# A hybrid encoder block on one core: one chunk of the residual turned by DMA, and a rotation in two halves

## The chip, the core and the metric

The kernel runs on one core of a Trainium2 chip. Its engines work side by side, each through its own list of instructions: TensorE (PE: matmuls, and transposes as matmuls with an identity), VectorE (DVE), ScalarE (ACT), GpSimd (POOL) and SyncE (SP, which here only issues DMAs). ACT and POOL can issue DMAs too. The metric is the device time of one execution in microseconds (us); less is better. A time is the median of several runs, and one more execution is profiled.

## The reference

One encoder layer in float32 over 512 tokens of width 2048:

```
h = rmsnorm(x);  qA|kA|vA|qB|kB|vB = h @ W_in
A = grouped-query attention, 8 heads, q and k normed and axially rotated
B = dilated sliding-window attention, 8 heads, q and k partially rotated:
    only the first 32 of a head's 128 columns are turned by the angles
x1 = x + concat(rmsnorm(A), rmsnorm(B)) @ W_out
out = rmsnorm(x1 + SwiGLU(rmsnorm(x1)))
```

What matters here: x1 (512 x 2048) is needed transposed, features on the partitions, as the operand of the gate-up matmul; and q and k of B are needed transposed for the scores.

## The kernel before

Every float32 matmul is three matmuls (`mm3`, L227 to L231) of a high and a low part: `split` writes the high part on ACT (a rounding copy) and the low part on DVE (the difference). Weights are split the same way, unit by unit: `split_hi` (L302) on ACT and `split_lo` (L307) on DVE; in the gate-up stage two units at once (L904, L907), with a sum of two weight tiles before it (L1040) for most forms, since that stage multiplies by a seven-product scheme (m1 to m7).

The program is written out by hand. Its order comes from a list of **units**: one unit is one weight tile times all 512 rows, 12 matmuls for the projections (a chunk of 512 output columns has 16 units, in the output projection 8), 6 for a unit of the gate-up stage. `prepare(n)` issues ahead of unit n the weight splits of a unit that comes later (in the output projection: the high part of unit n + 3, then the low part of unit n + 2). Work that belongs to no unit stands in a queue named `side`: after each unit `give` takes tasks from its head, and outside the attention a unit has a credit of 1.0, a task costs 1.0 unless it says otherwise, and `wait(k)` puts in k empty tasks. Every engine runs its instructions in the order in which they are issued this way.

**Output projection of B.** Four chunks c = 0 to 3 of eight units. The document counts them U0 to U31, so chunk 0 ends in U7, chunk 1 in U15, chunk 2 in U23, chunk 3 in U31; the gate-up stage follows with G0, G1 and so on (G0 is what U32 would be). At the end of a chunk `post` (L1187) adds the four row tiles to x1 on DVE (L1192), squares them on ACT (L1144, not for chunk 3), and puts the chunk's tasks into `side`. For chunks 0 to 2 these are `h_side(i, part)` for two pairs of feature blocks, i = 2c and 2c + 1:

- part 0 and part 1: four transposes of 128 x 128 on PE (L1238) into a PSUM bank, then a copy with the gain on ACT into `hpart[0]` (L1241); part 1 also forms four sums on DVE (`pair_sums`, L380);
- part 2: the split of seven forms, two copies on ACT (L1249) and two differences on DVE (L1251), into the arena that the gate-up matmuls read.

`park_x1(c)` stores the chunk from SP. Chunk 3's tasks are finer: parts 2 and 3 are the copy and the difference. Before the change the tasks of chunk 0 fall to U9 to U14 after two empty ones, those of chunk 1 to U16 to U21, those of chunk 2 to U24 to U29, and those of chunk 3 start in G0. The gate-up stage reads pair q as m1, q = 0 to 5 in G0 to G5, as m2, q = 0 to 5 in G6 to G11, then m1, q = 6 and 7 in G12 and G13.

**Turning by DMA.** Some heads are turned by `class Turned` without PE: `part(t)` separates on ACT the 16-bit halves of a row tile (L551, into `plane`), `turn(t)` transposes them by a DMA on SP's queue (L556, into `words`), `merge(h)` puts the halves together again on ACT (L561). They are used for heads 2 to 7 of A and heads 4 to 7 of B; B's heads come in pairs j, so these are pair groups j = 2 and 3.

**Rotation.** `rope_partial` (L533) rotates a whole pair group with four DVE instructions (L538 twice, L541, L542). Heads are worked in slots; head h of B starts at slot s = 4(8 + h). For j = 2 and 3 the group is reloaded from DRAM at slot s - 15, rotated at s - 11, and its row tiles are turned from s - 10 on. During the attention a unit's credit is higher, and `prepare`, `head_slot` and these tasks share the engines with the output projection of A.

Of the kernel before, what the change touches and what calls it, by code (L numbers as in the profile page):

```python
# [11 lines left out]
F32 = mybir.dt.float32  # L12
# [8 lines left out]
P = 128  # L21
# [45 lines left out]
COLUMN_BLOCKS = 3  # L67
SUM_LEAD = 6
ATTEND_PAST = 4
TURNED_ON_PE = {"A": 2, "B": 4}  # L70


# [5 lines left out]
def encoder_block(ctx, tc, x, w_in, g_q_a, g_k_a, w_out, w_gate_up, w_down, g_final, x_t, gains, c_ident, c_mask,  # L78
# [11 lines left out]
    def nm(base):  # L90
        counter[0] += 1
        return f"{base}_{counter[0]}"

    def slot(base, dtype=F32, shape=(P, 512)):
        return sp.tile(list(shape), dtype, tag="s", name=nm(base))
# [224 lines left out]
    def wait(n):  # L320
        side.extend([lambda: None] * n)
# [56 lines left out]
    def form_sums(a_l, a_r, b_l, b_r, s1, s2, s3, s4):  # L378
        def tt(out, x, y, op=OP.subtract):
            nc.vector.tensor_tensor(out, x, y, op=op)  # L380
        tt(s1, a_r, b_r, OP.add)
        tt(s3, a_l, a_r)
        tt(s2, s1, a_l)
        tt(s4, b_l, s2)
# [112 lines left out]
    def reload(name, dst):  # L497
        assert stored[name] == NT, name
        whole = slot(name, F32, (P, NT, 512))
        nc.sync.dma_start(whole, spill[name].rearrange("t p c -> p t c"))  # L500
        dst.update((t, whole[:, t]) for t in range(NT))
        dst["whole"] = whole
# [27 lines left out]
    def split_vB(h):  # L530
        vB[h] = split(vB[h].rearrange("p t c -> p (t c)"), "v", at=heads[NHA + h].home("v"))

    def rope_partial(q):  # L533
        rot = q.rearrange("p t (h d) -> p t h d", h=4)[:, :, :, :PARTIAL]
        tmp = turning.rearrange("p (t h c) -> p t h c", t=NT, h=4)
        hp = PARTIAL // 2
        for s in range(2):
            nc.vector.tensor_tensor(  # L538
                tmp[:, :, :, s * hp:(s + 1) * hp], rot[:, :, :, (1 - s) * hp:(2 - s) * hp],
                ropeb[:, 1, :, s * hp:(s + 1) * hp][:, :, None, :].to_broadcast([P, NT, 4, hp]), op=OP.mult)  # L540
        nc.vector.tensor_tensor(rot, rot, ropeb[:, 0][:, :, None, :].to_broadcast([P, NT, 4, PARTIAL]), op=OP.mult)  # L541
        nc.vector.tensor_tensor(rot, rot, tmp, op=OP.add)  # L542

    class Turned:
# [5 lines left out]
            src = self.whole()[:, t].bitcast(U16).rearrange("p (h c s) -> p h s c", h=4, s=2)  # L550
            nc.scalar.activation(p.rearrange("p (h s c) -> p h s c", h=4, s=2), src, AF.Copy)  # L551

        def turn(self, t):
            if self.words is None:
                self.words = slot("words", U16, (P, NT, 8, P))
            nc.sync.dma_start_transpose(self.words[:, t], self.planes.pop(t))  # L556

        def merge(self, h):
            m = slot("merged")
            src = self.words[:, :, 2 * h:2 * h + 2].rearrange("p t s c -> p t c s")  # L560
            nc.scalar.activation(m.bitcast(U16).rearrange("p (t c s) -> p t c s", c=P, s=2), src, AF.Copy)  # L561
            return m

    turned_a = [Turned(lambda j=j: qA[j]["whole"]) for j in range(2)]
# [167 lines left out]
    def weighed(cost, f):  # L732
        f.cost = cost
        return f

    def light(cost, tasks):
        return [weighed(cost, f) for f in tasks]

    def attention_tasks():
        def q_tasks(j):  # L740
            return norm_rope(lambda t: (qA[j][t], qA[j][t]), 4, "q")

        def both(cost, *lists):
            return [weighed(cost, lambda fs=fs: [f() for f in fs]) for fs in zip(*lists)]

        qA.update({j: {} for j in range(2)})
        qkB.update({j: {} for j in range(4)})
        push_heads()
        k_squares, k_turned, k_scaled = norm_rope(lambda t: (kA[t][:, :256], kA[t][:, 256:]), NKV, "k")
        q_squares, q_turned, q_scaled = q_tasks(0)  # L750
        vs = [lambda t=t: split_vA(t) for t in range(NT)]
        tables = light(0.8, table_tasks())
        todo = tables[:3] + both(1.4, [lambda t=t: scale_k(t) for t in range(NT)], k_squares)
        todo += both(0.6, vs) + tables[3:]
        todo += both(2.0, q_squares, k_turned, k_scaled) + both(2.6, q_turned, q_scaled)
        todo += light(0.6, [lambda kv=kv: transpose_k_a(kv) for kv in range(NKV)]) + [heads[0].tq, heads[0].tk]
        todo += light(0.1, [lambda: reload("qA1", qA[1])])
        extra = {}

        def at(slot, tasks):  # L760
            extra.setdefault(slot, []).extend(tasks)
        at(20, light(0.1, [lambda: nc.sync.dma_start(mask, c_mask)]))
        q_squares, q_turned, q_scaled = q_tasks(1)
        for t in range(NT):
            at(t // 2, both(0.8, q_squares[t:t + 1]))
            at(2 + 2 * t, both(0.9, q_turned[t:t + 1]))
            at(3 + 2 * t, both(0.9, q_scaled[t:t + 1]))
        def turn_at(turned, slots):
            for t, s in enumerate(slots):
                at(s, light(0.05, [lambda t=t: turned.part(t)]))  # L770
                at(s + 1, light(0.05, [lambda t=t: turned.turn(t)]))
        turn_at(turned_a[0], (0, 1, 2, 2))
        turn_at(turned_a[1], range(4, 12, 2))
        for j in range(4):
            s = NT * (NHA + 2 * j)
            lead = 4 if 2 * j >= TURNED_ON_PE["B"] else 0
            at(s - 11 - lead, light(0.1, [lambda j=j: reload(f"qkB{j}", qkB[j])]))
            at(s - 7 - lead, light(0.9, [lambda j=j: rope_partial(qkB[j]["whole"])]))
            if lead:
                turn_at(turned_b[j], range(s - 10, s - 6))  # L780
        for h in range(NHB):
            s = NT * (NHA + h)
            at(s + 2, light(0.1, [lambda h=h: load_vB(h)]))
            at(s + 4, light(0.4, [lambda h=h: split_vB(h)]))
        for s in range(2 * NHA * NT + VALUE_LAG + 2):
            cost = 1.5 if s < NHA * NT else 1.2 if s < 2 * NHA * NT else 0.7
            todo += [weighed(cost, lambda s=s: head_slot(s))] + extra.get(s, [])
        return todo
# [357 lines left out]
    def out_chunk(kind, c):  # L1146
# [28 lines left out]
        def mm(u, n):  # L1175
            k = order[n]
            if n == 0:
                box["ps"] = [bank() for _ in range(NT)]
                if kind == "A":
                    whole = slot("x1", F32, (P, NT, 512))  # L1180
                    x1[c] = [whole[:, t] for t in range(NT)]
                    for t in range(NT):
                        nc.sync.dma_start(x1[c][t], x[0, t * P:(t + 1) * P, c * 512:(c + 1) * 512])
            by_rows(u, n, NHA, lambda i, w, t: mm3(box["ps"][t], cols(oS[kind, order[i]], t * P), w, i == 0,
                                                   i == NHA - 1), post, kind == "A")

        def post(rows):  # L1187
            drain_until(lambda: kind in ro)
            if (kind, c) == ("B", 0) and 0 in rows:
                nc.scalar.activation(slot("table")[:, :1], ones, AF.Silu)  # L1190
            for t in rows:
                nc.vector.scalar_tensor_tensor(x1[c][t], box["ps"][t], ro[kind][:, t:t + 1], x1[c][t],  # L1192
                                               op0=OP.mult, op1=OP.add)
                release(box["ps"][t])
                if kind == "B" and c < NC - 1:
                    square_x1(c, t)
            if kind == "B" and NT - 1 in rows:
                wait(2 if c == 0 else 1)
                if c == NC - 1:
                    side.extend(lambda p=p: h_side(2 * c, p, True) for p in range(4))  # L1200
                    side.append(lambda: [square_x1(c, t) for t in (0, 1)])
                    side.extend(lambda p=p: h_side(2 * c + 1, p, True) for p in range(2))
                    side.append(lambda: park_x1(c))
                    side.append(lambda: [square_x1(c, t) for t in (2, 3)])
                    side.extend(lambda p=p: h_side(2 * c + 1, p, True) for p in range(2, 4))
                    side.append(make_r2)
                    return
                for i in (2 * c, 2 * c + 1):
                    for part in range(3):
                        side.append(lambda i=i, part=part: h_side(i, part))  # L1210
                side.append(weighed(0.0, lambda: park_x1(c)))
# [7 lines left out]
    def park_x1(c):  # L1219
        for t in range(NT):  # L1220
            nc.sync.dma_start(x1_dram[c, t], x1[c][t])

    def pair_sums(w):
        def part(n):
            return w[:, n * 256:(n + 1) * 256]
        a_r, a_l, s3, s2, b_l, b_r, s1, s4 = (part(n) for n in range(8))
        form_sums(a_l, a_r, b_l, b_r, s1, s2, s3, s4)

    hf = [False] * (KD // 2)
    hpart = {}  # L1230
# [465 lines left out]
```

## Time and profile before

| | us |
|---|---|
| median of 3 runs | 1950.06 (1948.17 to 1950.37) |
| the profiled execution | 1950.34, its span 1948.5 |
| PE busy | 1933.7 |
| DVE busy | 1536.4 |
| ACT busy | 1153.9 |
| POOL busy | 140.8 |

The span is what lies between the first and the last profiled instruction; 1.8 us of the profiled time lie around it. PE's granted clock was 0.999 of full. A row of a timeline gives the start, the duration, the engine, the line, the tiles written and read and, in square brackets, the engine's idle time before it with what ended it. A row of a line's or a tile's view gives the count and the shortest, median and longest duration in ns. A row of the waits gives the total in us, how often, and the longest. "SPq" and "ACTq" are those engines' issuing of DMAs.

### The profile page before, as it was taken

The numbers are of one execution on the slowest core, as the hardware profiler recorded it, in microseconds if no ns is written. First come the engines' busy times: TensorE is split into PE (matmuls) and PEld (weight loads), VectorE is DVE, ScalarE is ACT, GpSimd is POOL, SyncE is SP. The second block draws the span as 40 slices with busy tenths as digits, with TensorE's granted clock in tenths as the row PEclk, the third lists the DMA queues.
The fourth block names the chain that finished last, engine by engine and source line by source line (L and its number), as shares of the span: only waits on it lengthen the run. The fifth ranks groups of instructions, "written<-read, shape, count | busy, mean of one in ns | idle before, by whom it ended". The sixth has DMA issues, their size and how long they took to land.

```text
span 1948.5 us, 24527 instructions
## 1 busy us (share of the span) xinstructions
PE 1933.7 (99%) x8687; PEld 1594.9 (82%) x8687; DVE 1536.4 (79%) x2012; ACT 1153.9 (59%) x1673; POOL 140.8 (7%) x184
## 2 busy tenths in 40 slices
PE   9999999999999999999999999999999999999998
PEld 7888887888788888888888888888888888888886
DVE  7887768887785697778778777787788978787886
ACT  7655556676665565555555555555565666565555
POOL 0000011000000000000000000000000121111121
PEclk9999999999999999999999999999999999999999
DMA  9676694345442556758757778678587799868865
GB/s 347 221 276 218 214 295 112 100 168 161 115 150 95 183 185 215 272 148 280 244 173 275 222 206 286 186 240 291 144 287 264 217 239 272 229 164 242 236 145 170
DMA packets 268924, 413.50 MB, mean 212 GB/s; under 512 B 75584, under 2 KB 102720, under 8 KB 268672
## 3 DMA queue, kind: packets, MB, share of 16 engines
q1 hardware_dynamic: 237968, 325.31, 51.9%
q0 software_dynamic: 22480, 60.57, 12.4%
q10 hardware_dynamic: 8352, 26.05, 4.0%
q8 instruction: 68, 1.11, 0.2%
q14 instruction: 56, 0.46, 0.1%
HBM read 334.52 MB, written 62.65 MB: 204 GB/s over the span
## 4 chain that ended last, share of the span: by engine, by line
PE 87%; issue 8%; DVE 2%; ACT 1%; POOL 1%; DMA 0%; ACTq 0%; DVEq 0%; POOLq 0%; SPq 0%
PE b L230 29%; PE b L231 29%; PE b L229 29%; PE b L659 1%; DVE x L1192 0%; PE b L1238 0%; POOL fixed L211 0%; PE b L857 0%; POOL qkB L482 0%; DVE tw L963 0%; DVE w L307 0%; DMA stage<-in_w_in_dram 0%; DVE pair L380 0%; ACT rj L448 0%; ACT arena L1249 0%
## 5 line engine op out<-in xcount | busy, mean ns | idle before, releaser
L904 ACT ACTIVATE wide<-raw 128x1024 fp32r<-128x1024 f32 x462 | 487.3, 1059 | 456.9 <-PE b L231 264.8
L907 DVE TENSOR_TENSOR wide<-raw,wide 128x1024 fp32r<-128x1024 f32 x462 | 562.4, 1222 | 200.0 <-ACT wide L904 191.8
L229 PE MATMUL b<-wide,arena 128*128 128x512 f32 x1848 | 719.6, 389 | 0.0
L231 PE MATMUL b<-wide,arena 128*128 128x512 f32 x1848 | 719.0, 389 | 0.0
L230 PE MATMUL b<-wide,arena 128*128 128x512 f32 x1848 | 718.9, 389 | 0.0
L231 PEld LDWEIGHTS b<-wide,arena 128*128 128x128 f32 x1848 | 346.8, 188 | 72.0
L229 PEld LDWEIGHTS b<-wide,arena 128*128 128x128 f32 x1848 | 346.9, 188 | 72.0
L230 PEld LDWEIGHTS b<-wide,arena 128*128 128x128 f32 x1848 | 346.9, 188 | 71.7
L1040 DVE TENSOR_TENSOR raw<-raw,raw 128x1024 f32<-128x1024 f32 x264 | 321.4, 1219 | 9.3 <-DMA raw<-in_w_gate_up_dram 9.3
L230 PE MATMUL b<-tw,arena 128*128 128x512 f32 x396 | 154.3, 390 | 0.6 <-DVE tw L963 0.6
L231 PE MATMUL b<-tw,arena 128*128 128x512 f32 x396 | 154.1, 389 | 0.0
L229 PE MATMUL b<-tw,arena 128*128 128x512 f32 x396 | 154.1, 389 | 0.0
L960 ACT ACTIVATE tw<-stage 128x512 fp32r<-128x512 f32 x140 | 85.5, 629 | 69.3 <-DVE stage L1040 44.4
L963 DVE TENSOR_TENSOR tw<-stage,tw 128x512 fp32r<-128x512 f32 x140 | 93.7, 687 | 23.6 <-ACT tw L960 22.8
L229 PE MATMUL b<-w,arena 128*128 128x512 f32 x240 | 95.3, 397 | 0.0
L231 PE MATMUL b<-w,arena 128*128 128x512 f32 x240 | 93.9, 391 | 0.0
L230 PE MATMUL b<-w,arena 128*128 128x512 f32 x240 | 93.5, 390 | 0.0
L230 PEld LDWEIGHTS b<-tw,arena 128*128 128x128 f32 x396 | 74.3, 188 | 16.8 <-DVE tw L963 1.4
L229 PEld LDWEIGHTS b<-tw,arena 128*128 128x128 f32 x396 | 74.3, 188 | 15.6
L231 PEld LDWEIGHTS b<-tw,arena 128*128 128x128 f32 x396 | 74.3, 188 | 15.3
L380 DVE TENSOR_TENSOR pair<-pair 128x256 f32<-128x256 f32 x120 | 46.4, 422 | 46.8 <-ACT pair L1241 23.2
L1342 POOL DMA_DIRECT2D forms<-pair x22 | 20.1, 915 | 776.8 <-DVE pair L380 751.1
(243 smaller groups left out, 2138.3 us busy)
## 6 DMA issues: line engine op xcount, KB each, us to landing
raw<-in_w_gate_up_dram SPq DMA_DIRECT2D x308, 512.0 KB, 6.2
raw<-in_w_down_dram SPq DMA_DIRECT2D x88, 512.0 KB, 7.5
stage<-in_w_in_dram SPq DMA_DIRECT2D x111, 256.0 KB, 5.4
forms<-pair POOLq DMA_DIRECT2D x22, 896.0 KB, 6.3
fr<-forms ACTq DMA_DIRECT2D x35, 512.0 KB, 5.9
raw<-in_w_out_dram SPq DMA_DIRECT2D x32, 512.0 KB, 4.2
x1d<-s POOLq DMA_DIRECT2D x54, 256.0 KB, 6.8
stage<-in_w_in_dram SPq DMA_DIRECT2D x90, 128.0 KB, 3.5
```

Source lines behind the costliest of these rows:

```text
L229: nc.tensor.matmul(dst, ah, bh, start=start, stop=False, skip_group_check=chained)
L230: nc.tensor.matmul(dst, ah, bl, start=False, stop=False, skip_group_check=chained)
L231: nc.tensor.matmul(dst, al, bh, start=False, stop=stop, skip_group_check=chained)
L380: nc.vector.tensor_tensor(out, x, y, op=op)
L659: nc.tensor.transpose(ps[:, t * P:(t + 1) * P], self.p[t][:, kb * P:(kb + 1) * P], ident)
L904: nc.scalar.activation(self.hi, self.src, AF.Copy)
L907: nc.vector.tensor_tensor(self.lo, self.src, f32(self.hi), op=OP.subtract)
L960: nc.scalar.activation(self.pair[:, 0], self.src, AF.Copy)
L963: nc.vector.tensor_tensor(self.pair[:, 1], self.src, f32(self.pair[:, 0]), op=OP.subtract)
L1040: nc.vector.tensor_tensor(t[dst], t[src[0]], t[src[1]], op=OP.add if form == "m6" else OP.subtract)
L1342: nc.gpsimd.dma_start(forms_dram[:, :, n], hpart[0][:, 256:].rearrange("p (f c) -> p f c", c=256))
```

## The change

1. Pair groups j = 2 and 3 of B are reloaded one slot earlier (s - 16), and rotated in two halves of two heads each, at slots s - 13 and s - 12, with half the cost in credit each. Groups 0 and 1 stay as they were.
2. Chunk 0 of x1 is no longer transposed on PE. Its tasks are: one row tile a unit, separated on ACT and transposed by a DMA that ACT issues; the parking; then `half(0)` to `half(3)`, merges on ACT (for even halves in two pieces, so that the row tiles come in the order 2, 3, 0, 1) each followed by the scaled copy into `hpart[0]`, odd ones also by `pair_sums`; between them the splits `h_side(i, 2)`. The split of pair 0 and half 2 share a unit at 0.5 each.
3. The wait of two empty tasks moves from chunk 0 to chunk 1.

```
+X1_BY_DMA = 1
-    def rope_partial(q):
-        rot = q.rearrange("p t (h d) -> p t h d", h=4)[:, :, :, :PARTIAL]
-        tmp = turning.rearrange("p (t h c) -> p t h c", t=NT, h=4)
+    def rope_partial(q, lo=0, n=4):
+        rot = q.rearrange("p t (h d) -> p t h d", h=4)[:, :, lo:lo + n, :PARTIAL]
+        tmp = turning.rearrange("p (t h c) -> p t h c", t=NT, h=4)[:, :, lo:lo + n]
...
-        def turn(self, t):
+        def turn(self, t, queue=nc.sync):
...
-            nc.sync.dma_start_transpose(self.words[:, t], self.planes.pop(t))
+            queue.dma_start_transpose(self.words[:, t], self.planes.pop(t))
...
-        def merge(self, h):
-            m = slot("merged")
-            src = self.words[:, :, 2 * h:2 * h + 2].rearrange("p t s c -> p t c s")
-            nc.scalar.activation(m.bitcast(U16).rearrange("p (t c s) -> p t c s", c=P, s=2), src, AF.Copy)
+        def merge(self, h, runs=((0, NT),)):
+            m, at = slot("merged"), 0
+            for lo, hi in runs:
+                src = self.words[:, lo:hi, 2 * h:2 * h + 2].rearrange("p t s c -> p t c s")
+                dst = m[:, at:at + (hi - lo) * P].bitcast(U16)
+                nc.scalar.activation(dst.rearrange("p (t c s) -> p t c s", c=P, s=2), src, AF.Copy)
+                at += (hi - lo) * P
...
-            lead = 4 if 2 * j >= TURNED_ON_PE["B"] else 0
-            at(s - 11 - lead, light(0.1, [lambda j=j: reload(f"qkB{j}", qkB[j])]))
-            at(s - 7 - lead, light(0.9, [lambda j=j: rope_partial(qkB[j]["whole"])]))
-            if lead:
-                turn_at(turned_b[j], range(s - 10, s - 6))
+            if 2 * j < TURNED_ON_PE["B"]:
+                at(s - 11, light(0.1, [lambda j=j: reload(f"qkB{j}", qkB[j])]))
+                at(s - 7, light(0.9, [lambda j=j: rope_partial(qkB[j]["whole"])]))
+                continue
+            at(s - 16, light(0.1, [lambda j=j: reload(f"qkB{j}", qkB[j])]))
+            for n in range(2):
+                at(s - 13 + n, light(0.45, [lambda j=j, n=n: rope_partial(qkB[j]["whole"], 2 * n, 2)]))
+            turn_at(turned_b[j], range(s - 10, s - 6))
...
-                wait(2 if c == 0 else 1)
+                wait(2 if c == 1 else 1)
...
+                if c < X1_BY_DMA:
+                    side.extend(turned_x1(c))
+                    return
...
+    def turned_x1(c):
+        turned, i = Turned(lambda: x1["whole", c]), 2 * c
+        def row(t):
+            turned.part(t)
+            turned.turn(t, nc.scalar)
+        def half(j):
+            k = 4 * c + j
+            if not hpart:
+                hpart[0] = sp.tile([P, 4 * 512], F32, tag="pair", bufs=1, name=nm("pair"))
+            m = turned.merge(j, ((0, NT),) if j % 2 else ((2, NT), (0, 2)))
+            at = j % 2 * 1024
+            nc.scalar.activation(hpart[0][:, at:at + 512], m, AF.Copy, scale=gf[:, k:k + 1])
+            if j % 2:
+                pair_sums(hpart[0])
+        return [lambda t=t: row(t) for t in range(NT)] + [lambda: park_x1(c), lambda: half(0), lambda: half(1),
+                weighed(0.5, lambda: h_side(i, 2)), weighed(0.5, lambda: half(2)), lambda: half(3),
+                lambda: h_side(i + 1, 2)]
```

More of the change, by code (lines that the diff above doesn't have):

```diff
@@ L539, in rope_partial @@
                 tmp[:, :, :, s * hp:(s + 1) * hp], rot[:, :, :, (1 - s) * hp:(2 - s) * hp],
-                ropeb[:, 1, :, s * hp:(s + 1) * hp][:, :, None, :].to_broadcast([P, NT, 4, hp]), op=OP.mult)
-        nc.vector.tensor_tensor(rot, rot, ropeb[:, 0][:, :, None, :].to_broadcast([P, NT, 4, PARTIAL]), op=OP.mult)
+                ropeb[:, 1, :, s * hp:(s + 1) * hp][:, :, None, :].to_broadcast([P, NT, n, hp]), op=OP.mult)
+        nc.vector.tensor_tensor(rot, rot, ropeb[:, 0][:, :, None, :].to_broadcast([P, NT, n, PARTIAL]), op=OP.mult)
         nc.vector.tensor_tensor(rot, rot, tmp, op=OP.add)
@@ L1181, in mm @@
                     x1[c] = [whole[:, t] for t in range(NT)]
+                    x1["whole", c] = whole
                     for t in range(NT):
```

## The prediction

> **What bounds the kernel now.** I read the page's parts on busy time and on the chain first, then the waits of TensorE (PE), then the timelines of the places that the diff touches.
>
> ```profile
> span 1948.5 us, 24527 instructions
> PE 1933.7 (99%) x8687; PEld 1594.9 (82%) x8687; DVE 1536.4 (79%) x2012; ACT 1153.9 (59%) x1673; POOL 140.8 (7%) x184
> PE 87%; issue 8%; DVE 2%; ACT 1%; POOL 1%; DMA 0%; ACTq 0%; DVEq 0%; POOLq 0%; SPq 0%
> ```
>
> ```profile
> PE b L229 <- DVE pTl L221: 1.5, 2, 1.3
> PE b L659 <- DVE x L1192: 0.6, 1, 0.6
> PE b L1238 <- DVE x L1192: 0.5, 2, 0.3
> ```
>
> PE is busy for 1933.7 of 1948.5 us, and the chain of work that ended last runs 87% through it. A change can therefore win only by taking instructions off PE or by removing one of its few waits (the three above hold 2.6 us), and it loses whatever time it makes PE wait. VectorE (DVE) and ScalarE (ACT) count only where PE waits for them.
>
> **The turned chunk: what PE saves.** The transposes of L1238 stand between the matmuls:
>
> ```profile
> 613.04 0.60 PE L1238 MATMUL b<-fixed,x 128*128 128x128 f32 x4
> 616.25 0.60 PE L1238 MATMUL b<-fixed,x 128*128 128x128 f32 x4
> 619.44 0.39 PE L229 MATMUL b<-w,arena 128*128 128x512 f32 x1
> 622.16 0.60 PE L1238 MATMUL b<-fixed,x 128*128 128x128 f32 x4
> ```
>
> From 619.44 to 622.16 lie 12 matmuls, one output unit: 2.72 us, 0.227 each. From 613.04 to 616.25 lie 12 matmuls and one group of four transposes: 3.21 us. A group costs 0.49, and chunk 0 loses four: **-1.9 us**. Chunks 1 and 3 now wait for L1192 at their first transposes (the 0.5 above); the new order takes them to U20 and G2, four and two units later, when L1192 has ended: **-0.5**.
>
> **What ACT takes over.** The old path has an ACT row for every step but the DMA issue, which stands on SP:
>
> ```profile
> L551 ACT ACTIVATE plane<-qkB x8: 1042/1046/1064, 460.7 to 520.5; 128x1024 uint16<-128x1024 uint16 x8
> L556 SPq DMA_TRANSPOSE words<-plane x16: 1232/1239/1530, 324.9 to 521.6; - x16
> DMA to landing us min/median/max: 3.0/3.2/5.7
> L561 ACT ACTIVATE merged<-words x14: 1171/1188/1202, 339.9 to 555.9; 128x1024 uint16<-128x1024 uint16 x14
> L1331 ACT ACTIVATE pair<-turned x60: 670/684/1181, 788.9 to 1481.0; 128x512 uint16<-128x512 uint16 x40, 128x1024 uint16<-128x1024 uint16 x20
> 204.70 0.36 ACTq L482 DMA_DIRECT2D vB<-ends  x1
> 205.16 0.69 ACT L1088 ACTIVATE ends<-b,fixed 128x512 f32<-128x512 f32 x1 [0.49 <-ACT ends L1088]
> ```
>
> The last two rows show ACT issuing a DMA: it does nothing else until the issue is over and 0.1 us more. What a transpose costs there no row shows. The bounds are 0.33 (ACT's own plain DMAs) and 1.53 (the longest transpose issue on SP); I take SP's median of 1.24, since it is the same instruction and shape. Beside each unit's weight split (0.62 at 635.09 below, some 0.53 where two follow each other), a row tile then asks of ACT 0.53 + 1.05 + 1.24 + 0.13 = 2.95 us, against a unit of 2.72. Then come four merges (two as halves of 0.68 each, two of 1.19) and four scaled copies of some 0.65. Does that reach PE? The lines around chunk 1's end decide:
>
> ```profile
> 611.91 0.63 ACT L1144 ACTIVATE j<-x 128x512 f32<-128x512 f32 x1
> 612.54 1.14 ACT L302 ACTIVATE w<-raw 128x512 fp32r<-128x512 f32 x2
> 619.26 1.28 ACT L1249 ACTIVATE arena<-pair 128x1280 fp32r<-128x1280 f32 x1 [0.16 <-DVE pair L380]
> 620.57 1.49 DVE L1251 TENSOR_TENSOR arena<-pair,arena 128x1280 fp32r<-128x1280 f32 x1 [0.20 <-ACT arena L1249]
> 626.73 1.56 DVE L380 TENSOR_TENSOR pair<-pair 128x256 f32<-128x256 f32 x4 [3.47 <-ACT pair L1241]
> 631.29 0.39 PE L229 MATMUL b<-w,arena 128*128 128x512 f32 x1
> 631.71 2.72 DVE L1192 SCALAR_TENSOR_TENSOR x<-b,fixed,x 128x512 f32<-128x512 f32 x4
> 634.34 0.69 DVE L307 TENSOR_TENSOR w<-raw,w 128x512 fp32r<-128x512 f32 x1
> 635.09 0.62 ACT L302 ACTIVATE w<-raw 128x512 fp32r<-128x512 f32 x1
> ```
>
> The side queue gives one task of cost 1 a unit, so I count: U7 wait; U8 to U11 the row tiles; U12 park; U13 half 0; U14 half 1 with its sums (L380); U15 the split of feature pair 0 (L1249, L1251) and half 2; U16 half 3; U17 the split of pair 1. Before, pair 1's split stood in U14, ahead of chunk 1's end in U15. Now pair 0's split stands behind it. In the order of the program the split of U18's weights (L307) comes next on DVE, and U19's weights come behind the sums of pair 1.
>
> Take ACT first as if it were on time, and E as the end of U15 on PE (631.29 above). The squares end at E+3.8 (635.09); L1249's two copies (0.6 and 1.28) at E+5.7; L1251 at E+7.2; U18's split at E+7.9. PE wants it at E+5.4, two units after E: a stall of **2.4**. Behind it ACT merges half 2, copies it once L1251 is through (E+7.9), splits for U19 (E+8.4), merges and copies half 3 (E+10.2); DVE sums to E+11.8 and splits U19's weights by E+12.4, where PE would be at E+10.6: **1.8** more. So 4.2 us follow with no backlog at all.
>
> With the backlog: ACT's squares of chunk 0 end at 612.54, four row tiles at 2.95 end at 624.3, and the last transpose, issued at 623.0, lands 3.2 us later at 626.2. The merges of half 0 wait for it. With halves 0 and 1, their copies and two splits ACT is at 630.4; the sums end at 632.0, and U17's split, behind them, at 632.6. E is now 631.29 less four groups of 0.49, 629.3, so U17 should start at 632.0: a stall of 0.5. L1192, behind the same sums, ends at 635.3, the squares at 636.0, L1249 at 637.9, L1251 at 639.4, U18's split at 640.1; PE is ready at 635.3. That is 4.8 in place of 2.4. Together 0.5 + 4.8 + 1.8 = 7.1, from which I take 0.2 off because U18's first matmul needs no low part: **+6.9**. If the transpose lands only after 4.7 us (the median of the gate-up stage's own transposes), each number behind it is 1.5 later, 8.4; with an issue of 0.33 and landing hidden it is 4.2.
>
> ```profile
> turned<-pair SPq DMA_TRANSPOSE x40, 4.7
> ```
>
> [...]
>
> **Two units later in the gate-up stage.** Chunk 0's tasks end in U17 instead of U14, chunk 1's (two waits, six tasks) in U25 instead of U21, chunk 2's in U32 (that is G0) instead of U29, and chunk 3's list starts in G1 instead of U31, two units later. So the last split (pair 7) is issued in G12, where it was in G10. It is needed in G13 (m1, q = 7).
>
> ```profile
> 690.75 0.60 PE L1238 MATMUL b<-fixed,x 128*128 128x128 f32 x4
> 693.58 1.22 DVE L1040 TENSOR_TENSOR raw<-raw,raw 128x1024 f32<-128x1024 f32 x1
> 694.72 1.22 DVE L907 TENSOR_TENSOR wide<-raw,wide 128x1024 fp32r<-128x1024 f32 x1
> 698.13 2.26 DVE L1251 TENSOR_TENSOR arena<-pair,arena 128x512 fp32r<-128x512 f32 x2
> 699.38 0.39 PE L229 MATMUL b<-wide,arena 128*128 128x512 f32 x1
> ```
>
> The group at 690.75 is pair 7's second, after G6; 36 matmuls later, at 699.38, G13 starts. The part of L1251 that m1 reads, its first, was done at 698.13 + 2.26 - 1.49 = 698.9: 0.5 us to spare. Two units are 2 x 6 x 0.227 = 2.7 us; DVE, which works some 2.3 of them for other units (L1040 and L907, 1.14 each from start to start), has no time to catch up. 698.9 + 2.7 - 699.4 = 2.2 by the shift alone, 3.0 if a sum L1040 gets ahead of pair 7's sums, as the new order has it. I take **+2.6**; the range keeps 0 (DVE catches up in the gaps of the stage) and 3.0.
>
> **The rotation in halves.** Pair group 3 is rotated at 497.4:
>
> ```profile
> 490.34 0.69 DVE L221 TENSOR_TENSOR arena<-vraw,arena 128x512 fp32r<-128x512 f32 x1 [1.46 <-ACT arena L220]
> 496.18 0.69 DVE L224 SCALAR_TENSOR_TENSOR arena<-merged,arena 128x512 fp32r<-128x512 f32 x1 [1.37 <-ACT arena L223]
> 497.38 0.76 DVE L538 TENSOR_TENSOR rotary<-qkB,rotary 128x256 f32<-128x256 f32 x2
> 499.51 1.40 DVE L1192 SCALAR_TENSOR_TENSOR x<-b,fixed,x 128x512 f32<-128x512 f32 x2
> 503.97 0.50 PE L229 MATMUL b<-arena 128*128 128x512 f32 x1 [1.30 <-DVE pTl L221]
> 505.54 0.66 PE L659 MATMUL b<-fixed,p 128*128 128x128 f32 x4 [0.60 <-DVE x L1192]
> ```
>
> The four instructions take 499.51 - 497.38 = 2.1 us of DVE right ahead of L1192 of an output chunk, and PE waits 1.30 and 0.60 behind them. One and two slots earlier DVE idles 1.46 and 1.37, about what a half (four shorter instructions, 1.1 to 1.5 together) needs. The first wait goes; the second is for rows that PE itself finishes late, so I count half of it: **-1.6** (0 to -1.9). Group 2 moves two slots ahead too; no whole rotation but group 3's has a wait of PE behind it in the list above, so I take 0 for its halves, up to +0.5. The reload now stands three slots ahead of its first use, at the 6 us between 490.34 and 496.18 some 17 us, against 5.4 to landing; at half that pace it still holds.
>
> ```profile
> qkB<-qkB SPq DMA_DIRECT2D x4, 1024.0 KB, 5.4
> ```
>
> **The sum.** -1.9 - 0.5 - 1.6 + 6.9 + 2.6 = +5.5 us. The profiled execution took 1950.34 for its span of 1948.5, 0.28 above the median of 1950.06. 1950.06 + 5.5 = **1955.6**.
>
> **The rivals.**
> - *The cover holds* (the other side): split ahead by three units, PE never sees ACT's burst. Place: U18's split on DVE. It decides at 5.4 us after U15's end; if L1251 is through by E+4.7, only the gains stay: -4.0, 1946.1. For it: ACT is busy for only 59% of the span. Against: 3.8 us of squares and 3.4 of pair 0's split lie in one line behind E. Chance 0.15.
> - *One stall of the two*: G13's split in time, or ACT's issue as short as 0.33. 5.5 - 2.6 = +2.9 or 5.5 - 2.7 = +2.8, both together +0.2: 1950.3 to 1953.0. Chance 0.21.
> - *Worse*: the landing takes 4.7, or ACT waits for some other transfer: +1.5 to +4, 1957 to 1960. The stall near 5 us can also cost PE its clock. The opening shows what that is:
>
> ```profile
> 5.15 5.10 PE L857 MATMUL b<-tw,arena 128*128 128x512 f32 x12 [0.72 <-DVE tw L1612]
> ```
>
> Twelve matmuls in 5.10 us after a wait, 0.425 each against 0.227. If that came back for eight matmuls after the stall it would add 8 x 0.2 = 1.6 us, 1957.2. [...] Chance of all these together 0.14.
> - *As summed*: 1953.0 to 1958. Chance 0.50.
>
> **The numbers.** Some 0.2%, 3.9 us, is what a measurement can tell from no change: faster is under 1946.2, slower over 1954.0. Slower holds "as summed" but for its low end, and "worse": 0.60. "The cover holds" lies on the border: 0.10 of it faster, the rest same, with the single stalls and that low end 0.30. The range 1946 to 1960 takes in the single stalls, the unknown landing and issue on ACT and the upper half of the cover that holds; it leaves out some 0.1.
>
> **What would show it.** L1238 with 48 instead of 64; DMA_TRANSPOSE on ACT's queue with its duration; new waits of PE for L307 in U17 to U19 and for L1251 at G13; the waits for pTl L221 and L1192 near 504 gone. If PE shows no wait for L307 there, the count of the side tasks or ACT's pace is wrong and the time falls to 1946; if the L307 waits are there and G13's is not, DVE caught up.

## The result and the profile after

The changed kernel takes **1958.14 us** (median of 4 runs, 1957.23 to 1960.69) against 1949.96 of the kernel before beside it: a ratio of 1.0045, with a 95% interval from 1.0034 to 1.0057. It is slower by 8.2 us; the forecast was +5.5. The profiled execution took 1957.23 for a span of 1955.4.

The first two lines are from the page of the changed kernel. The others are from its list of TensorE's waits (total us, times, longest).

```profile
span 1955.4 us, 24535 instructions
PE 1935.0 (99%) x8671; PEld 1594.0 (82%) x8671; DVE 1537.6 (79%) x2020; ACT 1161.2 (59%) x1683; POOL 140.6 (7%) x184
```

```profile
PE b L231 <- DVE w L308: 4.2, 1, 4.2
PE b L230 <- ACT arena L1280: 1.9, 1, 1.9
...
PE b L663 <- DVE x L1200: 1.2, 2, 0.6
PE b L231 <- DVE wide L914: 0.7, 1, 0.7
...
PE b L232 <- DVE arena L1282: 0.4, 1, 0.4
```

The lines have moved down: L308 is the low split of the weights (L307 before), L1280 and L1282 the split of a feature pair (L1249, L1251), L1200 the rows of x1 (L1192), L1269 the transposes (L1238), L914 the low split of the gate-up weights (L907). PE has 16 matmuls fewer and yet is busy for longer. Each of the two largest waits is new, and each stands where the forecast put one.

**U18.** First ScalarE's row tiles of chunk 0, then what follows the end of chunk 1, from the timelines of ACT, DVE and PE of the changed kernel:

```profile
610.84 1.04 ACT L552 ACTIVATE plane<-x 128x1024 uint16<-128x1024 uint16 x1
611.91 1.33 ACTq L557 DMA_TRANSPOSE words<-plane  x1
613.28 0.63 ACT L303 ACTIVATE w<-raw 128x512 fp32r<-128x512 f32 x1 [1.40 <-issue]
...
620.70 1.25 ACTq L557 DMA_TRANSPOSE words<-plane  x1
...
623.77 0.69 ACT L564 ACTIVATE merged<-words 128x512 uint16<-128x512 uint16 x1 [0.62 <-DMA words<-plane]
...
631.03 0.63 ACT L1151 ACTIVATE j<-x 128x512 f32<-128x512 f32 x1 [2.36 <-DVE x L1200]
...
633.64 1.77 ACT L1280 ACTIVATE arena<-pair 128x512 fp32r<-128x512 f32 x2
```

```profile
628.18 1.55 DVE L381 TENSOR_TENSOR pair<-pair 128x256 f32<-128x256 f32 x4 [4.22 <-ACT pair L1253]
...
630.25 2.72 DVE L1200 SCALAR_TENSOR_TENSOR x<-b,fixed,x 128x512 f32<-128x512 f32 x4
...
635.44 1.49 DVE L1282 TENSOR_TENSOR arena<-pair,arena 128x1280 fp32r<-128x1280 f32 x1 [0.47 <-ACT arena L1280]
636.86 0.68 DVE L308 TENSOR_TENSOR w<-raw,w 128x512 fp32r<-128x512 f32 x1
```

```profile
630.39 0.50 PE L231 MATMUL b<-w,arena 128*128 128x512 f32 x1
...
637.59 0.79 PE L231 MATMUL b<-w,arena 128*128 128x512 f32 x1 [4.19 <-DVE w L308]
638.18 0.63 PE L232 MATMUL b<-w,arena 128*128 128x512 f32 x1
638.61 0.63 PE L230 MATMUL b<-w,arena 128*128 128x512 f32 x1
```

Read it backwards from 637.59. PE waits for U18's low split (636.86); that stands in DVE's order behind pair 0's differences (635.44), these wait for pair 0's copies on ACT (633.64), and these stand behind the four squares of chunk 1 (from 631.03). The "2.36 <- x L1200" ahead of the squares says that ACT was idle before them, but this is no time that the chain could have used: the squares need x1's rows, and DVE came to these only at 630.25, 3.1 us after the end of U15 (627.13; in the kernel before 0.4, 631.71 against 631.29). Ahead of them stood U17's split and the sums of half 1 (628.18), for which DVE had waited 4.22 us, since ACT's merges began only when the last transpose had landed (623.77). So both parts that the forecast named are there, the backlog from chunk 0 and the line of work behind U15.

U17 lost some time too: its second matmul, the first that needs a low part, starts at 630.39 instead of 630.08, just behind its split (ended at 630.33).

From 638.18 on the matmuls start every 0.43 us instead of every 0.227. The windows of the same run, cut at the edges where the rate changes (PE busy, count, then its granted clock), show it whole:

```profile
632.20:635.60 3.40, 1.21 (x6) 0.99 0.32 110
635.60:639.00 3.40, 1.41 (x3) 0.50 0.02 5
639.00:642.40 3.40, 3.40 (x9) 0.50 0.00 0
642.40:645.80 3.40, 3.40 (x16) 1.00 0.67 142
```

The clock falls to 0.50 while PE still waits, and stays there until 642.4. The wait costs 4.2 us; the first matmul and ten more at half rate cost (0.59 - 0.227) + 10 x 0.2 = 2.4 on top. From the start of U16 (627.13) to that of U20 (645.19) are 18.06 us, where four units of 2.72 would take 10.88: 7.2 lost in all, 0.4 of them in U17.

**G13**, pair 7's split, from the timeline and the windows (busy time and count of PE, PE's weight loads, DVE, ACT and POOL, then the granted clock):

```profile
703.27 0.50 PE L230 MATMUL b<-wide,arena 128*128 128x512 f32 x1 [1.85 <-ACT arena L1280]
...
704.40 0.80 PE L232 MATMUL b<-wide,arena 128*128 128x512 f32 x1 [0.36 <-DVE arena L1282]
```

```profile
700.46:703.87 3.41, 1.56 (x7) 0.76 (x5) 3.41 (x4) 3.41 (x7) 0.00 (x0) 0.99 1.04 351
703.87:707.28 3.41, 3.05 (x8) 2.30 (x8) 3.31 (x6) 2.55 (x4) 1.01 (x1) 0.51 0.49 160
```

The longer wait is for ACT's copies of pair 7, the shorter for DVE's differences. The third matmul of G13 starts 2.7 us late (704.40; due 0.227 x 3 behind 701.03, the start of the last one of G12), and the matmuls at half rate until 707.28 cost another 1.4.

**What was gained.** The group of L1269 counts 48 transposes where L1238 had 64, and no wait for x stands before them any more. In the attention the 1.30 us wait for pTl is gone, but the 0.60 for x1's rows stayed, and one like it came where there was none:

```profile
L1269 PE MATMUL b<-fixed,x x48: 270/272/273, 647.9 to 695.7; 128*128 128x128 f32 x48
```

```profile
502.19 0.66 PE L663 MATMUL b<-fixed,p 128*128 128x128 f32 x4 [0.60 <-DVE x L1200]
...
539.83 0.66 PE L663 MATMUL b<-fixed,p 128*128 128x128 f32 x4 [0.60 <-DVE x L1200]
```

One difference has nothing to do with the change. The twelve opening matmuls, 5.10 us in the profiled run before, took 3.00 here:

```profile
4.98 3.00 PE L864 MATMUL b<-tw,arena 128*128 128x512 f32 x12 [0.65 <-DVE tw L1643]
```

**The account.** Leave the transposes of x1 out of both lists of PE's matmuls: each then has 8623, and at the places below the n-th of one does the work of the n-th of the other. Their starts, in us:

| matmul | before | after | after less before | what made the step from the row above |
|---|---|---|---|---|
| ahead of the rotation of group 3 | 446.39 | 444.71 | -1.68 | the opening, -1.7 |
| behind it | 574.04 | 571.82 | -2.22 | the rotation, -0.5 |
| first of U16 | 631.29 | 627.13 | -4.16 | four groups of transposes, -1.9 |
| last of G12 | 699.15 | 701.03 | +1.88 | U16 to G12, +6.0 |
| first of G15 | 702.10 | 708.12 | +6.02 | G13 and G14, +4.1 |
| last of the kernel | 1940.04 | 1947.15 | +7.11 | a wait for wide L914 at 1502, +1.1 |

The +6.0 are the 7.2 lost in U17 to U19, less 1.1 for the waits for x1's rows that are gone: in the kernel before, the first groups of chunks 1 and 3 cost 0.9 and 1.2 us, the other groups not quite 0.5. The rotation gains 0.5, not 1.6.

So the two profiled spans (+6.9) flatter the change by 1.7 us, the opening. The last section comes back to that.

### The profile page after: what moved, and what is told of

Read it like the earlier page. It is cut to its first block, busy times and chain, and to the rows that moved or that the text cites. A ratio compares the mean times of both kernels' runs of the same rounds, so it can differ in the third digit from the quotient of the medians.

```text
span 1955.4 us, 24535 instructions
## 1 busy us (share of the span) xinstructions
PE 1935.0 (99%) x8671; PEld 1594.0 (82%) x8671; DVE 1537.6 (79%) x2020; ACT 1161.2 (59%) x1683; POOL 140.6 (7%) x184
## 5 line engine op out<-in xcount | busy, mean ns | idle before, releaser
L914 DVE TENSOR_TENSOR wide<-raw,wide 128x1024 fp32r<-128x1024 f32 x462 | 562.8, 1223 | 204.0 <-ACT wide L911 191.8
L221 ACT ACTIVATE pTh<-b 128x512 fp32r<-128x512 f32 x64 | 38.3, 598 | 64.4 <-PE b L663 62.5
```

Of the source, the lines that this page charges most:

```text
L221: nc.scalar.activation(hi, src, AF.Copy)
L914: nc.vector.tensor_tensor(self.lo, self.src, f32(self.hi), op=OP.subtract)
```

## The experiments

The main theory: PE waits for weight splits on DVE, which stand behind a burst of ACT and DVE (at U18), and for a pair 7 that comes two units late (at G13), and each wait is followed by a stretch at half rate. The rivals: the DMA transposes, or their issue by ACT, cost something as such; the rotation in halves has its part in the loss. Experiments 1 to 4 ran on one chip and 5 to 11 on another; the kernel before, run beside them, took 1949.66 to 1949.93 us on both. The names in brackets are those that the expectations use.

**1. The rotation alone.** (`e1_rope_only`) The kernel before with the rotation of the change, and `X1_BY_DMA = 0` (wait of two back at chunk 0).

> The kernel before with the rotation in two halves alone (reload at s-16, halves at s-13 and s-12); chunk 0 of x1 is turned on TensorE as before. Prediction on record: -1.6 us of 1950 (0 to -1.9). The trace of the changed kernel, where the 1.30 us wait is gone but a 0.60 us wait has come at another place, says only about -0.3 us. So: main theory (the loss of the change is all in chunk 0) -0.3 to -1.6 us against before, all at the two first turned tiles; rival (the halves, with more and shorter VectorE instructions, cost time somewhere) +1 us or more.

1948.17 us (11 runs, 1947.77 to 1949.99) against 1949.93; ratio 0.9994 (0.9985 to 1.0003). It loses nothing and gains less than can be told. Its list of waits shows the same exchange as the changed kernel's: no 1.30 for pTl, two waits of 0.6 for x1's rows. Between the first two matmuls of the account PE comes 0.56 us further ahead of the kernel before in its trace, and 0.03 in that of experiment 2, which lacks the halves: the rotation is worth some 0.5 us, too little for these runs.

**2. The turned chunk alone.** (`e2_x1_only`) The changed kernel with the old rotation:

```
-            at(s - 16, light(0.1, [lambda j=j: reload(f"qkB{j}", qkB[j])]))
-            for n in range(2):
-                at(s - 13 + n, light(0.45, [lambda j=j, n=n: rope_partial(qkB[j]["whole"], 2 * n, 2)]))
+            at(s - 15, light(0.1, [lambda j=j: reload(f"qkB{j}", qkB[j])]))
+            at(s - 11, light(0.9, [lambda j=j: rope_partial(qkB[j]["whole"])]))
```

> The changed kernel with the old rotation (one rotation per tile, reload at s-15): chunk 0 by DMA alone. Main theory: the PE stalls of 4.2 us at U18 and 1.9 + 0.4 us at G13 and the half-rate matmuls after each stay, so +8 to +9 us against before, 0 to 1 us slower than the changed kernel. Rival (the rotation in halves carries a part of the loss): under +6 us against before.

1958.88 us (1955.84 to 1959.36), ratio 1.0042 (1.0028 to 1.0056), with the changed kernel's two stalls:

```profile
PE b L231 <- DVE w L308: 4.4, 2, 4.2
PE b L230 <- ACT arena L1279: 1.8, 1, 1.8
```

The whole loss comes with chunk 0; the rival on the rotation is out.

**3. The squares later.** (`e3_squares_later`) Chunk 1's squares leave the end of U15 and fill its two empty tasks:

```
-                if kind == "B" and c < NC - 1:
+                if kind == "B" and c < NC - 1 and c != 1:
...
-                wait(2 if c == 1 else 1)
+                if c == 1:
+                    side.extend(lambda r=r: [square_x1(1, t) for t in r] for r in ((0, 1), (2, 3)))
+                else:
+                    wait(1)
```

> The changed kernel; chunk 1's four squares on ScalarE leave the end of U15 and go, two and two, into its two empty tasks (U16 and U17's places). Theory 1 (U18's stall is the wait for its low split on VectorE, which stands behind the splitting of pair 0 on ScalarE, which stands behind the four squares, 4 x 0.63 us): the splits of pair 0 start about 2.5 us sooner, the stall at U18 falls from 4.2 to about 2 us, -2 to -4 us against the changed kernel, by how much of the half-rate stretch goes with it; G13's stall stays. Rival (the DMA_TRANSPOSEs issued by ScalarE are what delays, whatever stands behind them): the stall stays over 3.5 us.

1955.06 us (1953.29 to 1956.23), ratio 1.0026 (1.0017 to 1.0036): 3.1 under the changed kernel.

```profile
PE b L231 <- DVE w L308: 2.4, 2, 2.2
PE b L230 <- ACT arena L1283: 1.9, 1, 1.9
```

The wait at U18 is 2.2 instead of 4.2, by the 2.0 that were expected, with the same transposes issued by ACT ahead of it. The squares were in its way.

**4. The splits of five units sooner.** (`e4_ahead`) `ahead` is how far in front of a unit, in us of PE's time, its weights are split; it was 10.0.

```
+                if tag == "wo" and pieces[0][0] == 1024 and i < 5:
+                    units[-1].ahead = 13.1
```

> The changed kernel; the weight splits of U16 to U20 alone are made one to two units earlier, so that U18's low split stands ahead of x1's rows of chunk 1 and of pair 0's low splits on VectorE. ScalarE's and the DMA's work of chunk 0 is the same. Theory 1 (the loss at U18 is the order on VectorE): the 4.2 us wait at U18 and the half-rate matmuls after it go, the granted clock there is 1.00 again, -4 to -6.5 us against the changed kernel, so +2 to +4 against before, and G13's stall (1.9 + 0.4 us and its slow matmuls) stays. Rival (transposes by DMA during U9 to U12, or contention, slow the whole stretch): less than -2 us.

1958.04 us (1956.68 to 1958.34), ratio 1.0041 (1.0029 to 1.0054): nothing gained, so the expectation of the main theory failed. From the timelines of PE and DVE:

```profile
644.42 0.79 PE L231 MATMUL b<-w,arena 128*128 128x512 f32 x1 [6.20 <-DVE w L308]
```

```profile
642.27 1.49 DVE L1284 TENSOR_TENSOR arena<-pair,arena 128x1280 fp32r<-128x1280 f32 x1 [0.79 <-ACT arena L1282]
643.68 2.49 DVE L308 TENSOR_TENSOR w<-raw,w 128x512 fp32r<-128x512 f32 x4
```

PE ran through U18 and U19 and met a wait of 6.20 at U20: low parts are issued one unit behind the high parts, so U20's low part, the last of the five, was only issued with U21's high part, behind the whole of pair 1. With the splits of U18 and U19 out of the line, the next one waits at its end. That fits both the theory (order) and its rival (the engines are full there), so the same was done for the whole chunk.

**5. The splits of all eight units of chunk 2 sooner** (`e4b_chunk_ahead`) (`i < 8`).

> As e4_ahead, but for all eight units of chunk 2 (U16 to U23). In e4_ahead the 4.2 us wait at U18 went and one of 6.2 us came at U20, whose low split still stood behind pair 1's, so nothing was gained. Here U20's and U21's stand ahead of pair 1's splitting too. Theory 1 (PE waits for whichever weight split stands behind the pairs of chunk 0 on ScalarE and VectorE; with all of them ahead of the pairs the same work costs nothing): the stalls in U16 to U23 fall to under 2 us in sum, worked out from the rows of e4_ahead (U20's split at 637.1 once pair 0's is done, needed at 638.1; pair 1's end at 643.7, U22 needed at 643.5), time -4 to -6.5 us against the changed kernel, +2 to +4 against before; G13's stall stays. Rival (the burst moves the stall wherever the splits stand, since the engines are full): under -2 us, a stall over 3 us at U21 or U22.

1951.29 us (1948.98 to 1952.51), ratio 1.0007 (0.9998 to 1.0016): 6.8 under the changed kernel, a little more than expected.

```profile
PE b L230 <- ACT arena L1282: 1.8, 1, 1.8
...
PE b L231 <- DVE w L308: 0.7, 1, 0.7
```

In place of 4.2 at U18 stands 0.7 at U21. ACT and DVE do the same work in the same stretch, the transposes by DMA are all there, and PE hardly sees it. The burst was affordable; the order was not.

**6. Both** (`e5_ahead_squares`) (5 with the squares of 3).

> e4b_chunk_ahead with chunk 1's squares later as in e3_squares_later. Theory 1: no stall is left in U16 to U23, the granted clock is 1.00 there, and only G13's stall and its slow matmuls remain (1.9 + 0.4 us and about 2): +0.5 to +2.5 us against before. Rival as there: a stall over 1 us stays in chunk 2 and the time is +3 us or more.

1951.65 us (1949.65 to 1953.07), ratio 1.0007 (0.9998 to 1.0016). No wait for L308 is left in the list. In its trace PE comes to G13 3.5 us ahead of the kernel before; G13's stall with its half rate takes 4.6 and a wait for the gate-up weights 0.7, which leaves +1.8 at the end, as the medians have it (+2.0). The squares add nothing once the splits are ahead.

**7. Without the empty tasks of chunks 2 and 3** (`e6_no_waits`) (6, and `wait(1)` for chunk 0 alone).

> e5_ahead_squares without the one empty task ahead of chunk 2's and chunk 3's pairs, so that pair 7 is split two units earlier. Theory 1 (G13's stall is the two units by which chunk 0's longer list of tasks pushes pair 7): G13's stall and its slow matmuls go, -3 to -4.5 us against e5_ahead_squares; with the four transpose groups saved and the rotation in halves that is -1 to -3.5 us against before, unless PE now waits at chunk 3's transposes for x1 (then 0 to +2). Rival (the DMA transposes cost something that no stall shows): at before's time or above although the two stalls are gone.

1948.83 us (1946.73 to 1949.63), ratio 0.9994 (0.9986 to 1.0003): 2.8 under 6. G13's wait and its half rate are gone (granted clock 1.00 from 698 to 712 us), so it was the two units. Part of the gain goes to a new wait, at chunk 3's transposes, which now come before x1's rows are there:

```profile
PE b L1274 <- DVE x L1202: 1.8, 2, 1.5
```

**8. The transposes from SyncE.** (`e7_sp_queue`) `turned.turn(t)` in place of `turned.turn(t, nc.scalar)` in the changed kernel.

> The changed kernel with chunk 0's four DMA_TRANSPOSEs issued by SyncE instead of ScalarE. ScalarE is then 4 x 1.25 us less busy during U9 to U13. Theory 1 (the loss is made after U15, by the order of the splits, not by the issuing): ScalarE had 2.4 us to spare ahead of the squares of chunk 1 anyway, so the stalls at U18 and G13 stay within 0.5 us of 4.2 and 1.9 and the time within 1 us of the changed kernel, unless SyncE's issues hold up weight loads queued behind them (then slower). Rival (issuing on ScalarE is what the change pays for): -3 us or more against the changed kernel.

1955.55 us (6 runs, 1953.85 to 1959.48), ratio 1.0036 (1.0024 to 1.0049); the interval overlaps the changed kernel's. The profiled run has both stalls:

```profile
PE b L231 <- DVE w L308: 3.5, 1, 3.5
PE b L230 <- ACT arena L1280: 1.8, 1, 1.8
```

The wait at U18 is 0.7 shorter, a little more than the theory allowed, and the median 2.6 lower, more than the 1 it allowed and less than the rival's 3. ACT, free of the issues, only waited for the data instead, 5.30 us:

```profile
623.97 1.27 ACT L564 ACTIVATE merged<-words 128x512 uint16<-128x512 uint16 x2 [5.30 <-DMA words<-plane]
```

```profile
637.80 0.80 PE L231 MATMUL b<-w,arena 128*128 128x512 f32 x1 [3.50 <-DVE w L308]
```

PE is due at U18 at 637.80 - 3.50 = 634.30 here, 10.3 us behind the first merge; in the changed kernel at 637.59 - 4.19 = 633.40, 9.6 behind it. So the issuing by ACT makes 0.7 us of the stall of 4.2; the rest of the difference in the profiled run is half rate, five matmuls at U18 and none at G13 (granted clock 0.89 from 630 to 646 us, 1.00 from 698 to 712). Issuing on ACT is the smaller part of what the change pays for; how much of the 2.6 between the medians is its own and how much the half rate's, these six runs do not tell.

**9. The squares of chunk 3 first** (`e9_squares_first`) (7, and two of chunk 3's squares ahead of its first transposes).

```
+                    side.append(lambda: [square_x1(c, t) for t in (0, 1)])
                     side.extend(lambda p=p: h_side(2 * c, p, True) for p in range(4))
-                    side.append(lambda: [square_x1(c, t) for t in (0, 1)])
```

> e6_no_waits with two of chunk 3's four squares on ScalarE ahead of chunk 3's first transposes instead of behind the pair of them, so that TensorE comes to these transposes a unit of gate-up (1.36 us) later and pair 7 is split no later. In e6_no_waits TensorE waited 1.52 + 0.27 us there for x. Theory 1: that wait falls to under 0.5 us and nothing comes in its place, -1 to -1.8 us against e6_no_waits, -1.5 to -3.5 against before. Rival (a wait moved is a wait found elsewhere): within 0.5 us of e6_no_waits, with a new wait of over 1 us.

**1947.02 us** (11 runs, 1945.95 to 1948.05), ratio 0.9987 (0.9979 to 0.9996) against 1949.9: 2.9 us under the kernel before, and faster than both kernels. The wait of 1.8 is 0.4:

```profile
PE b L1274 <- DVE x L1202: 0.4, 2, 0.3
```

**10. The same with chunk 0 on TensorE** (`e10_none_turned`) (`X1_BY_DMA = 0` in 9).

> e9_squares_first with chunk 0 turned on TensorE, as before, and everything else kept: what turning chunk 0 by DMA is worth once its stalls are gone. Theory 1 (the four transpose groups of 0.49 us were all that TensorE could save): e9_squares_first is 1.4 to 2.4 us faster than this one, and this one -1 to +1 against before. Rival (the DMA turning still loses what it saves): this one is as fast as e9_squares_first or faster.

1953.14 us (1951.8 to 1956.22), ratio 1.0021 (1.0012 to 1.003): 6.1 over 9, where 1.4 to 2.4 was expected, and 3.2 over the kernel before, where at most 1 was.

```profile
PE b L1274 <- DVE x L1202: 3.8, 4, 2.4
```

The comparison isn't clean. Chunk 0's own transposes have one empty task ahead of them instead of two, and without chunk 0's long list those of chunk 2 have none: PE waits 1.1 us for x1 at the first and 2.7 at the other, 3.8 in all and 3.4 more than in 9. What is left, 2.7, is near the four groups of 0.49 and 0.7 over them. The kernel before gives a cleaner measure: from the second matmul of the account to the fifth, experiment 9 comes 2.2 us further ahead of it, 1.9 of them by the third. Empty tasks that look like waste were cover.

**11. How a wait slows what follows.** (`e8_delays`) The kernel before, with k reductions added in nine gate-up blocks:

```
+        if f0 // 4 in DELAYS:
+            def delay(k=DELAYS[f0 // 4]):
+                for _ in range(k):
+                    nc.vector.tensor_reduce(junk, ident.rearrange("p (a c) -> p a c", a=4), axis=AX.X, op=OP.add)
+            box.after("m6", 4, delay)
```

> The kernel before with VectorE reductions of 128x128 added in nine gate-up blocks (12, 18, 24, 30, 36, 21, 27, 33 and 42 of them), to make PE wait there for splits by graded times; nothing of the computation is changed. Read: the length of each PE wait against the matmuls at half rate behind it and the granted clock. Theory (half rate follows a gap of about 2 us or more and lasts some 4 us whatever its length): gaps under 1 us are followed by none, gaps over 2 us by 6 to 12 matmuls at 0.43 us. Rival (it grows with the gap): the number of slow matmuls is in proportion to the wait.

One run, 2016.9 us. From PE's timeline, three of the nine waits:

```profile
880.10 0.50 PE L231 MATMUL b<-wide,arena 128*128 128x512 f32 x1 [2.90 <-DVE wide L908]
1216.76 0.80 PE L231 MATMUL b<-wide,arena 128*128 128x512 f32 x1 [3.88 <-DVE wide L908]
1475.67 0.79 PE L231 MATMUL b<-wide,arena 128*128 128x512 f32 x1 [10.61 <-DVE wide L908]
```

From the starts of the matmuls behind each wait:

| wait, us | matmuls spaced 0.43 after it | full rate again at |
|---|---|---|
| 0.98 | 0 | |
| 2.90 | 0 | |
| 4.83 | 12 | 967.36 |
| 6.77 | 11 | 1052.71 |
| 8.69 | 5 | 1138.03 |
| 3.88 | 6 | 1219.94 |
| 5.79 | 10 | 1305.33 |
| 7.73 | 7 | 1390.63 |
| 10.61 | 7 | 1479.35 |

The number does not grow with the wait (8.69 has fewer than 3.88), so the rival is out. The theory was roughly right, but 2.90 had none, while the changed kernel's 1.85 + 0.36 had some: the length alone does not decide. How these waits lay is in the last section.

## Why the prediction was right, and its time 2.5 us low

- **The place and the chain at U18: right.** The profiled run came to U16 2.2 us ahead of the forecast's clock, 1.7 by its opening, by chance, and 0.5 by the rotation, which that clock left out. With 2.2 taken off, the forecast has the end of U15 at 627.1 (measured 627.13), the last transpose issued at 620.8 (620.70), the squares ended at 633.8 (633.6), pair 0's copies at 635.7 (635.4), differences at 637.2 (636.9), U18's split at 637.9 (637.5); stall 4.8 (4.19). Experiments 3 and 5 confirm each end of it: take the squares out and it shortens by 2.0, take the splits out of the line and it goes.
- **The issue on ACT at 1.24: right** (1.25 to 1.33), and the landing at 3.2 (at most 3.1 from the last issue to the first merge).
- **"Together 7.1, less 0.2": the sum right, in part by luck.** U17 lost 0.4 (0.5 forecast) and U18's wait was 4.2 (4.8). U19's 1.8 did not come: at half rate PE spent 2.4 us more on what followed the wait, so U19's low split, ended at 641.9, was in time for 642.4. At full rate PE would have been there at some 640.3 (637.59 and 12 matmuls of 0.227; an estimate) and would have waited: the half rate took the place of a stall, and the 7.2 measured against 6.9 hides that.
- **G13: the place and the shift right, its price short.** PE came 2.7 us late to the third matmul, the first that needs a low part of pair 7 (DVE), where 2.6 was forecast; but the longer of its two waits was for ACT's copies, which the forecast did not name, and 1.4 of half rate came on top: 4.1. Experiment 7 removes it by removing the two units.
- **Half rate: wrongly left to a rival.** "Worse" gave it 1.6 us after a stall near 5; it came after both stalls and cost 2.4 + 1.4 in the profiled run. The sum put it at nothing. That it comes behind a stall inside the stream, and for eight matmuls, was the author's estimate from the opening; the changed kernel had eleven slow matmuls at U18 and six at G13.
- **The rotation: over-sized.** -1.6 in the sum, -0.5 measured: the 1.30 went, the 0.60 stayed whole, since PE now came to x1's rows sooner, and a wait of 0.60 with a slow restart behind it (the second matmul 0.32 us after the first, not 0.227) came at the next chunk. Experiment 1 bears it out with a gain too small to tell.
- **The transposes: -1.9 right, -0.5 under-sized.** Four groups gave 1.9. The two waits for x1's rows held 0.5 us, but the groups that they stood in cost 0.9 and 1.2 where the others cost not quite 0.5: 1.1 more.
- **Not foreseen:** a wait of 0.74 for wide L914 at 1502 us, 1.1 with what follows it. Waits of 0.2 to 0.8 for that line's tile stand in the traces of experiments 2 to 4 and 6 to 8 as well and not in those of 1, 5, 9 and 10; why was not followed up.

The sum as measured: -1.9 - 1.1 - 0.5 + 7.2 + 4.1 + 1.1 = +8.9. The profiled spans give the same, 6.9 and 1.7 for the opening, to 0.3; between the medians lie 8.2.

## What to carry to other kernels

Ask of a moved task not only what engine time it takes but what it now stands in front of: here the engines had the time (the same work costs nothing in experiment 5), and the loss was a weight split queued behind a burst. Whoever lengthens a hand-made queue should go through everything behind it and see whose due time that passes, here pair 7, two units later; and empty tasks in such a queue may be cover (experiments 7 and 10). Price a wait of TensorE with the stretch at half rate that can follow it: in the changed kernel 2.4 us behind the wait of 4.19 and 1.4 behind that of 1.85, but none behind 1.84 in experiment 4 or 2.90 in experiment 11.

## What the runs showed of the hardware

**The ends of half rate lie whole multiples of 3.41 us apart.** In the changed kernel the granted clock is at 0.50 from 635.56 to 642.39 and from 703.83 to 707.24 us, for 6.83 and 3.413 us, and 61.44 lie between the two: 2, 1 and 18 times 3.413. In experiment 11 the half rate ended at 967.36, 1052.71, 1138.03, 1219.94, 1305.33, 1390.63 and 1479.35 us. The steps between them are 85.35, 85.32, 81.91, 85.39, 85.30 and 88.72: 25, 25, 24, 25, 25 and 26 times 3.413, to 0.1 us.

**One stall, followed by half rate in one run and by none in another.** G13's stall is in the changed kernel and in experiment 4 the same to 0.03 us. From the timeline and the windows of experiment 4, cut in steps of 3.413 us from the end of its half rate (649.94; 16 windows on is 704.55):

```profile
704.91 0.50 PE L230 MATMUL b<-wide,arena 128*128 128x512 f32 x1 [1.84 <-ACT arena L1282]
...
706.04 0.50 PE L232 MATMUL b<-wide,arena 128*128 128x512 f32 x1 [0.39 <-DVE arena L1284]
```

```profile
646.53:649.94 3.41, 3.41 (x11) 0.50 0.78 287
649.94:653.35 3.41, 3.41 (x19) 1.00 0.47 154
701.14:704.55 3.41, 1.93 (x9) 1.00 1.04 372
704.55:707.97 3.42, 2.66 (x10) 1.00 0.72 232
```

Here the 1.84 us lie across an edge, 1.48 in one window and 0.36 in the next (0.75 with the 0.39), and the clock stays at 1.00: no half rate. In the changed kernel the 1.85 lie inside one window (700.46 to 703.87, busy 1.56), and the next is at 0.51. The 2.90 of experiment 11 was halved by an edge too (878.6), 1.40 and 1.50, and had no slow matmul.

The traces before and after can be cut the same way between the opening and the end, in steps of 3.413 us from the first record of a full clock before (9.70) and from 642.39 after. Two windows of the changed kernel at full clock have PE idle for 2.15 and 1.85 us (from 632.15 and 700.42), and each is followed by one at half rate. In the others the most is 1.30 before (from 501.22) and 0.74 after, and none is. At half rate, a window with 2.03 us idle (changed kernel, from 635.56) and one with 0.96 (experiment 11, from 960.50) were followed by another; those with 0.00 and 0.36 (changed kernel, from 638.98 and 703.83) were the last. That the place of a wait against these edges decides is the author's inference from these cases; no run was made to test it.

**Two openings, and two groups of times.** The twelve opening matmuls took 5.10 us in the profiled run before and 3.00 in that of the changed kernel, which opens with the same instructions; 3.01 in experiment 1 and 5.27 in experiment 9. Of the 11 traces before, after and of experiments 1 to 3 and 5 to 10, four show 47 to 49 matmuls in the first 15 us and seven 40 to 43, none a number between. The times of the kernel before fall into two groups: of 21 runs beside experiment 9, 7 lie from 1948.14 to 1948.69 and 14 from 1949.62 to 1950.47. That the groups are the two openings is argued from the profiled runs (1950.34 with a slow one); the other runs have no trace.
